# Feed-forward of a transformer block: a gate quad's seventh product behind the second product of what follows, and all products in one order

## The chip, the cores and the metric

The kernel runs on one core of a Trainium2 chip. The metric is the device time of one execution in microseconds (us), lower is better. Runs are told as a median with the lowest and the highest, and one execution is taken by the hardware profiler.

## The reference

The kernel computes one pre-norm encoder block for 2048 tokens of width 1024: a combined projection, two kinds of attention, an output projection, and a SwiGLU feed-forward of width 2816. The change is in the feed-forward alone, which is this part of the reference:

```
D_FF = ((8 * D_MODEL + 3 * 256 - 1) // (3 * 256)) * 256        # 2816
...
    u2 = rms_norm(h, norm2_w[l])
    gate = jnp.einsum('bsd,df->bsf', u2, w_gate[l])
    up = jnp.einsum('bsd,df->bsf', u2, w_up[l])
    h = h + jnp.einsum('bsf,fd->bsd', jax.nn.silu(gate) * up, w_down[l])
```

## The kernel before

Matrix products run on TensorE in f16, each operand split into a high and a low half, so that one product of two split blocks is three matmuls for each block of the contraction. A 2 by 2 block product is done with seven products and a chain of additions (Strassen's scheme in Winograd's form) and not with eight.

**The feed-forward's steps.** The tokens are two halves of 1024, the width 2816 is 11 groups of 256, so there are 22 steps (half, group), numbered 0 to 21 here. A step is a gate quad (`gate`, seven products of the step's gate weights `wg`), then an up quad (`up`, seven products of `wu`). Every product of a quad is 12 matmuls of 128x512 (`product`). Two steps after they were begun, two groups are multiplied into the result (`down`, "units"): this happens between the gate and the up of steps 2, 4, 6, 8, 10, then at step 11 for the single last group of the first half, then at steps 13, 15, 17, 19; the last three groups come at the end. A `down` has four blocks of 256 tokens (`j`), each with seven products of three matmuls for every unit, so 6 matmuls for two units. Its additions go into tiles `hs` (or `stages`) that are loaded from `hd` in memory (`load_hs`) and stored back there.

**Order of a quad.** With the names of `quad`: `pa` (first product), `p6`, `p7`, `pd`, a second product added into `pa`, `p4`, and the seventh, added into `pd`. Behind each stands an addition on VectorE or a copy on ScalarE: L1043, L1047, L1052, L1057 (reads `pd` after its first product), L1067, L1071 (reads `pd` after the seventh). The seventh can start when L1057 has read `pd`. A silu (L1083) in a gate, and L1103 in an up, follow. `hooks(n)` is called after the n-th product and advances the loading of weights.

**Loading of weights in the first half** (`load_ffn`, a generator that the hooks advance; in the second half ready weights are read back from memory): a DMA into one of two `stages`; ScalarE squares it into the one buffer `sq` (L954 for gate and up weights, L190 for down weights); a short group of matmuls, tile `fsc` (L963, or L183 through `across`), takes the sums over the partitions; VectorE makes the scale of them (L964, L175 to L205); then ScalarE, GpSimd and VectorE write the high and low halves (L216, L98, L221). The buffer `sq` is also the room for two combined blocks (`mix`), so the next square waits until L221 has read them. The up weights' `fsc` is traced at the gate's hook 2, the next step's gate weights' square at the gate's hook 6 and their `fsc` at its hook 7.

**PSUM.** Products and `fsc` tiles get their bank from `pst`, which counts: every fourth tile is of a pool of two, the other three of a pool of six.

**Who sets the order.** The program is traced as above, and then a list scheduler with a timeline of its own orders each engine's instructions: among those that it holds ready it takes the earliest traced, so a later product may be put ahead of an earlier one. `tc.issue_after(ins)` adds an edge: what the block traces on the engine of `ins` is issued behind `ins` (order only, no wait for its end). Before the change only the helpers (`fsc`, transposes `xtr`) carry such an edge, by `with behind():`, to `front[0]`, the last product's matmul traced so far; products carry none.

The changed functions and their callers:

Of the kernel before, what the change touches and what calls it, by code (L numbers as in the profile page):

```python
# [16 lines left out]
ALU = mybir.AluOpType  # L17
# [4 lines left out]
S, D, P = 2048, 1024, 128  # L22
# [18 lines left out]
CU = 3  # L41
# [18 lines left out]
def block(tc, a, out):  # L60
# [3 lines left out]
    with top:  # L64
# [64 lines left out]
        half = c1(2, "half")  # L129
# [744 lines left out]
        with ExitStack() as ph2:  # L874
# [150 lines left out]

            def product(ps_, wv, wo, X, xo, start, stop):
                q = 0
                for kt in range(4):
                    for xi, wi in ((0, 0), (1, 0), (0, 1)):
                        front[0] = PE.matmul(ps_[:].rearrange("p (t n) -> p t n", n=P), lhsT=wv[:, wo, wi, 128 * kt : 128 * kt + 128], rhs=X[xo][:, :, xi, kt, :], start=start and q == 0, stop=stop and q == 11, skip_group_check=not start).ins  # L1030
                        q += 1

            def quad(wv, X, tag, bufs, c11, hooks):
                def at(n):
                    hooks(n)

                def cst():
                    return fp.tile([P, 512], F32, tag=tag, bufs=bufs, name=nm(tag))

                pa = pst("pa")  # L1040
                product(pa, wv, 0, X, 0, True, True)
                u2 = cst()
                ACT.copy(u2[:], pa[:])  # L1043
                at(1)
                p6 = pst("pm")
                product(p6, wv, 4, X, 4, True, True)
                DVE.tensor_tensor(u2[:], p6[:], u2[:], ALU.add)  # L1047
                at(2)
                p7 = pst("pm")
                product(p7, wv, 6, X, 5, True, True)  # L1050
                u3 = cst()
                DVE.tensor_tensor(u3[:], p7[:], u2[:], ALU.add)  # L1052
                at(3)
                pd = pst("pd")
                product(pd, wv, 2, X, 2, True, True)
                c22 = cst()
                DVE.tensor_tensor(c22[:], pd[:], u3[:], ALU.add)  # L1057
                c11(1, 1, c22)
                at(4)
                product(pa, wv, 1, X, 1, False, True)  # L1060
                c11(0, 0, pa)
                note("D", 3000)
                note("A", 500)
                at(5)
                p4 = pst("pm")
                product(p4, wv, 3, X, 6, True, True)
                DVE.tensor_tensor(u3[:], u3[:], p4[:], ALU.subtract)  # L1067
                c11(1, 0, u3)
                at(6)
                product(pd, wv, 5, X, 3, False, True)  # L1070
                DVE.tensor_tensor(u2[:], u2[:], pd[:], ALU.add)  # L1071
                c11(0, 1, u2)
                at(7)

            def gate(W, X, hooks):
                sg = {}

                def on_gate(f, t, c):
                    if (f, t) == (0, 0):
                        s = fp.tile([P, 512], F32, tag="cg", bufs=5, name=nm("cg"))  # L1080
                    else:
                        s = c
                    ACT.activation(s[:], c[:], AF.Silu, scale=W["kg"][:])  # L1083
                    sg[f, t] = s

                quad(W["g"], X, "cg", 5, on_gate, hooks)
                note("A", 2000)
                return sg

            def up(W, X, sg, hooks, final=False):  # L1090
                if final:
                    act = stages[:].rearrange("p b n -> p (b n)").bitcast(F16)[:, :7168].rearrange("p (o s n) -> p o s n", o=7, s=2)
                else:
                    act = fp.tile([P, 7, 2, 512], F16, tag="act", bufs=2, name=nm("act"))

                def put(o, src):
                    ACT.copy(act[:, o, 0], src)  # L1097
                    note("A", 500)
                    tt(act[:, o, 1], src, act[:, o, 0], ALU.subtract, 512, LE)

                def on_up(f, t, c):
                    s = sg[f, t][:]
                    DVE.scalar_tensor_tensor(s, c[:], W["F"][:], s, op0=ALU.mult, op1=ALU.mult)  # L1103
                    if (f, t) != (0, 1):
                        put({(0, 0): 0, (1, 0): 1, (1, 1): 3}[f, t], s)
                        return
                    a11, a12, a21, a22 = (sg[k][:] for k in ((0, 0), (1, 0), (0, 1), (1, 1)))
                    s3 = fp.tile([P, 512], F32, tag="cu", bufs=CU, name=nm("cu"))
                    tt(s3[:], a11, a21, ALU.subtract, 512, SE)
                    tt(a21, a21, a22, ALU.add, 512, SE)  # L1110
                    put(2, a21)
                    tt(a11, a21, a11, ALU.subtract, 512, SE)
                    tt(a12, a12, a11, ALU.subtract, 512, SE)
                    put(6, a12)
                    put(4, a11)
                    put(5, s3[:])

                quad(W["u"], X, "cu", CU, on_up, hooks)
                note("D", 2440)
                return act  # L1120

# [6 lines left out]
                    SP.dma_start(h[q][:], hd[8 * half + 2 * j + q])  # L1128
                return h

            def down(half, units, hs, last, hook=None):
                kd = units[-1][0]["kd"]
                nu = len(units)

                def prod(po, ao, wo, j, start=True):
                    for u, (W, act) in enumerate(units):
                        for q, (xi, wi) in enumerate(((0, 0), (0, 1), (1, 0))):
                            front[0] = PE.matmul(po[:], lhsT=act[:, ao, xi, 128 * j : 128 * j + 128], rhs=W["d"][:, wo, wi, :], start=start and u == 0 and q == 0, stop=u == nu - 1 and q == 2, skip_group_check=not start).ins  # L1138

                def ust():  # L1140
                    return fp.tile([P, 512], F32, tag="cu", bufs=CU, name=nm("cu"))

                def acc(dst, po, src):
                    DVE.scalar_tensor_tensor(dst, po[:], kd[:], src, op0=ALU.mult, op1=ALU.add)  # L1144

                def first(j):
                    pa = pst("pd")
                    prod(pa, 0, 0, j)
                    return pa

                ahead = [first(j) for j in range(4)] if nu == 3 else []
                for j in range(4):
                    if j == 2 and hook is not None:
                        hook()
                    if j + 1 < 4:
                        hs.append(load_hs(half, j + 1, nu == 3, last))
                    h0, h1 = hs[j]
                    c11, c12, c21, c22 = h0[:, :512], h0[:, 512:], h1[:, :512], h1[:, 512:]
                    note("D", 3600)
                    note("A", 500)  # L1160
                    ae = "D" if last and j == 3 else AE
                    pa = ahead.pop(0) if ahead else first(j)
                    u2 = ust()
                    ACT.mul(u2[:], pa[:], kd[:])
                    pb = pst("pd")
                    prod(pb, 4, 4, j)
                    acc(u2[:], pb, u2[:])
                    pc = pst("pd")
                    prod(pc, 5, 6, j)
                    u3 = ust()  # L1170
                    acc(u3[:], pc, u2[:])
                    tt(c12, c12, u2[:], ALU.add, 512, ae)
                    pd = pst("pd")
                    prod(pd, 2, 2, j)
                    prod(pa, 1, 1, j, False)
                    acc(c22, pd, c22)
                    prod(pd, 6, 3, j, False)
                    acc(c11, pa, c11)
                    pe = pst("pd")
                    prod(pe, 3, 5, j)  # L1180
                    acc(c12, pd, c12)
                    acc(c21, pe, c21)
                    tt(c21, c21, u3[:], ALU.add, 512, ae)
                    tt(c22, c22, u3[:], ALU.add, 512, ae)
                    for q in range(2):
                        t = 8 * half + 2 * j + q
                        SP.dma_start(out[t * P : (t + 1) * P, :] if last else hd[t], hs[j][q][:])
# [69 lines left out]
            for i, (half, fg) in enumerate(steps):  # L1257
# [48 lines left out]
                        go("u")  # L1306
                    row(7 + s)

                sg = gate(W, X, in_gate)
                if not more:  # L1310
                    load_now(half, fg, "d", W)
                if due:
                    down(dh, units, hs, dh != half, lambda: go("g"))
                    units = []
                act = up(W, X, sg, in_up, not more)
                if more and steps[i + 1][0] == 1:
                    go("u", 9)
                units.append((W, act))
# [27 lines left out]
```

## Time and profile before

| | |
|---|---|
| median of 3 runs | 2686.87 us |
| lowest to highest | 2677.16 to 2687.23 us |
| profiled execution, its time | 2682.59 us |
| profiled execution, its span | 2680.8 us |
| first matmul of the feed-forward (gate of step 0) | 1427.2 us from the span's start |
| first matmul of its second half (gate of step 11) | 2059.6 us |

In the rows, PE is TensorE, DVE VectorE, ACT ScalarE, POOL GpSimd, SP the queue of most DMAs. A row of the timeline has start and length in us, then engine, line, operation, output and inputs with buffer numbers left out, shapes and a count; in brackets the idle time of the engine ahead of it and what ended it. Tiles of a quad are named `pa`, `pm` (for `p6`, `p7`, `p4`) and `pd`; those of `down` are all `pd`, on L1138, with inputs `wd,act`. A row of the waits has who waited for whom, us in total, times, and the longest. A row of the windows has the stretch, its length, each engine's busy time and count in the order PE, PE's weight loads, DVE, ACT, POOL, then the granted clock, the share of the DMA engines and GB/s.

### The profile page before, as it was taken

The page shows a single profiled execution, that of the slowest core. Times are in us where ns is not written, and L with a number is a line of the kernel's source. Part 1 is how long each engine was busy: PE and PEld are TensorE (multiplying, and loading weights), DVE is VectorE, ACT ScalarE, POOL GpSimd, SP SyncE. Part 2 cuts the span into 40 slices and gives each one's busy share as a digit, 9 for nine tenths or more (in the row PEclk, how much of TensorE's full clock was granted, in tenths as well). Part 3 has the DMA queues.
Part 4 walks back from the last instruction along what each step waited for, and adds up shares of the span by engine and source line. Part 5 has one row for each costly group of instructions (what it writes and reads, how often), then busy time and mean ns, then how long its engine had stood idle before and what let it go on. Part 6 is the DMA issues. An engine that isn't in the chain of part 4 may idle for free. (4 is left out here: it accounts for less than half of the span.)

```text
span 2680.8 us, 50579 instructions
## 1 busy us (share of the span) xinstructions
PE 2492.4 (93%) x19628; PEld 1498.6 (56%) x19628; DVE 1932.7 (72%) x3711; ACT 1347.0 (50%) x2487; POOL 1489.1 (56%) x1098
## 2 busy tenths in 40 slices
PE   6998989888988989889989899999999999999999
PEld 4655656577776776557775344444444444444444
DVE  6898969898989989877766868777685544444434
ACT  4665656567978878665644535344352112111121
POOL 2578667667767766546764656565564232322323
PEclk9999999999999999999999899999999999999999
DMA  6777697767998979987897574665649743635532
GB/s 222 213 162 181 146 200 168 179 143 184 193 179 179 185 160 209 210 191 217 218 285 282 208 250 178 255 226 202 245 183 346 293 177 143 233 141 186 195 111 95
DMA packets 619585, 534.41 MB, mean 199 GB/s; under 512 B 480640, under 2 KB 548224, under 8 KB 609104
## 3 DMA queue, kind: packets, MB, share of 16 engines
q1 hardware_dynamic: 617520, 529.09, 69.9%
q8 instruction: 154, 2.52, 0.4%
q0 software_dynamic: 512, 1.36, 0.2%
q14 instruction: 87, 0.71, 0.1%
q10 hardware_dynamic: 1312, 0.72, 0.1%
HBM read 261.08 MB, written 147.32 MB: 152 GB/s over the span
## 5 line engine op out<-in xcount | busy, mean ns | idle before, releaser
L98 POOL TENSOR_TENSOR s<-z,s 128x1024 f16<-128x1024 f32 (+7 forms) x288 | 472.0, 1647 | 142.5 <-ACT s L89 109.8
L507 PE MATMUL sc<-kT,qT 128*128 128x512 f16 (+3 forms) x1520 | 382.0, 353 | 53.3 <-DVE z L623 19.3
L622 DVE TENSOR_TENSOR_SCAN z<-z,sc 128x512 f32<-128x512 f32 (+3 forms) x320 | 352.8, 1112 | 58.6 <-ACT sc L620 38.0
L1138 PE MATMUL pd<-wd,act 128*128 128x512 f16 x1764 | 390.9, 379 | 1.2 <-DVE cg L1071 1.2
L326 PE MATMUL pj<-w,xt 128*128 128x384 f16 x1920 | 352.2, 331 | 18.8 <-ACT xt L683 6.9
L1030 PEld LDWEIGHTS <-wg 128*128 128x128 f16 x1848 | 182.0, 99 | 230.2 <-issue 16.4
L518 PE MATMUL yp<-v,aT 128*128 128x64 f16 (+1 forms) x4896 | 269.8, 204 | 41.6 <-DMA aT<-s 40.2
L518 PEld LDWEIGHTS <-aT 128*128 128x128 f16 x4896 | 237.5, 99 | 120.4 <-DMA aT<-s 52.5
L1030 PEld LDWEIGHTS <-wu 128*128 128x128 f16 x1848 | 180.7, 98 | 218.0 <-issue 2.6
L98 POOL TENSOR_TENSOR act<-cg,act 128x512 f16<-128x512 f32 x112 | 148.5, 1337 | 262.9 <-ACT act L1097 150.8
L1138 PEld LDWEIGHTS <-act 128*128 128x128 f16 x1764 | 172.8, 98 | 209.4 <-issue 2.8
L326 PEld LDWEIGHTS <-xt 128*128 128x128 f16 x1920 | 187.3, 99 | 147.5 <-issue 21.4
L89 ACT CAST s<-z 128x128 f16<-128x128 f32 (+7 forms) x215 | 173.1, 809 | 134.1 <-DMA aT<-s 40.5
L98 POOL TENSOR_TENSOR hs<-hs,cu 128x512 f32<-128x512 f32 x99 | 130.9, 1328 | 171.3 <-DVE hs L1144 70.8
L619 ACT ACTIVATE z<-sc,c 128x512 f32<-128x512 f32 (+3 forms) x320 | 210.7, 663 | 25.6 <-PE sc L507 11.7
L1097 ACT CAST act<-cg 128x512 f16<-128x512 f32 x126 | 77.3, 616 | 238.4 <-DVE cg L1103 162.7
L507 PEld LDWEIGHTS <-qT 128*128 128x128 f16 x1520 | 128.4, 99 | 121.0 <-DVE z L623 23.0
L832 PE MATMUL po<-wo,mt 128*128 128x256 f16 x1536 | 180.7, 277 | 13.9 <-DVE xf L835 8.4
L1030 PE MATMUL pm<-X,wu 128*128 128x512 f16 x792 | 180.4, 379 | 1.3 <-DVE wu L221 1.3
L1030 PE MATMUL pm<-X,wg 128*128 128x512 f16 x792 | 181.3, 382 | 0.0
L342 PE MATMUL pj<-xt,w 128*128 128x128 f16 x2304 | 175.0, 220 | 6.7 <-DVE v L364 5.7
L1144 DVE SCALAR_TENSOR_TENSOR hs<-pd,c,hs 128x512 f32<-128x512 f32 x136 | 99.0, 747 | 109.6 <-PE pd L1138 83.1
(266 smaller groups left out, 4737.6 us busy)
## 6 DMA issues: line engine op xcount, KB each, us to landing
xt<-xs SPq DMA_DIRECT2D x112, 512.0 KB, 4.3
hs<-hd SPq DMA_DIRECT2D x68, 512.0 KB, 4.5
hd<-hs SPq DMA_DIRECT2D x56, 512.0 KB, 4.7
split<-wg SPq DMA_DIRECT2D x11, 1792.0 KB, 7.8
split<-wu SPq DMA_DIRECT2D x11, 1792.0 KB, 6.7
split<-wd SPq DMA_DIRECT2D x11, 1792.0 KB, 7.2
wg<-split SPq DMA_DIRECT2D x11, 1792.0 KB, 7.3
wd<-split SPq DMA_DIRECT2D x11, 1792.0 KB, 12.2
```

Source lines behind the costliest of these rows:

```text
L89: ACT.copy(dst, src)
L98: (DVE if e == "D" else POOL).tensor_tensor(dst, a_, b_, op)
L326: PE.matmul(pj[:, :384], lhsT=xv[:, xi, kt, :], rhs=G["w"][:, wi, kt, :], start=n == 0, stop=n == 23)
L342: PE.matmul(o, lhsT=x_ if c == 2 else w_, rhs=w_ if c == 2 else x_, start=n == 0, stop=n == 23)
L507: last = PE.matmul(sc[:, : 128 * w].rearrange("p (t n) -> p t n", n=P), lhsT=G["q"][i // 4][:, a_, i % 4, :], rhs=G["k"][q][:, b_, 0:w, :] ...
L518: PE.matmul(yp[:, y0 : y0 + wd], lhsT=aT[:, a_, :], rhs=v[:, v_ : v_ + wd], start=start and j == 0 and q == 0, stop=stop and j == nb - 1 a ...
L619: ACT.activation(om[:, lo:hi], sc[:, :w], AF.Sigmoid, scale=G["nkz"][:])
L622: DVE.tensor_tensor_scan(ov, ov, sc[:, :w], om[:, hi : hi + 1], op0=ALU.mult, op1=ALU.bypass)
L832: PE.matmul(po[:, sl], lhsT=mt[:, kt, P * xi : P * xi + P], rhs=wos[2 * h + n][wi][:, kt, :], start=q == 0, stop=q == 23)
L1030: front[0] = PE.matmul(ps_[:].rearrange("p (t n) -> p t n", n=P), lhsT=wv[:, wo, wi, 128 * kt : 128 * kt + 128], rhs=X[xo][:, :, xi, kt, : ...
L1138: front[0] = PE.matmul(po[:], lhsT=act[:, ao, xi, 128 * j : 128 * j + 128], rhs=W["d"][:, wo, wi, :], start=start and u == 0 and q == 0, s ...
L1144: DVE.scalar_tensor_tensor(dst, po[:], kd[:], src, op0=ALU.mult, op1=ALU.add)
```

## The change

`quad` hands out its seventh product as a function; with `late` (gates alone) it does not call it. The next `down` calls it at its first block `j == 0` behind its second product, or, in a step without one, the next `up` calls it behind its `p6`. Hook 7 of a gate is now called before the seventh product has been traced. Every product, of quads and of `down`, is traced inside `with behind():`, so each matmul of it has an edge to the last matmul of the product traced before it. The count of tiles in `pst` stays as it was.

```diff
             def product(ps_, wv, wo, X, xo, start, stop):
                 q = 0
-                for kt in range(4):
-                    for xi, wi in ((0, 0), (1, 0), (0, 1)):
-                        front[0] = PE.matmul(...).ins
-                        q += 1
+                with behind():
+                    for kt in range(4):
+                        for xi, wi in ((0, 0), (1, 0), (0, 1)):
+                            last = PE.matmul(...)
+                            q += 1
+                front[0] = last.ins
...
-            def quad(wv, X, tag, bufs, c11, hooks):
+            def quad(wv, X, tag, bufs, c11, hooks, before=None, late=False):
...
                 DVE.tensor_tensor(u2[:], p6[:], u2[:], ALU.add)
+                if before is not None:
+                    before()
                 at(2)
...
                 at(6)
-                product(pd, wv, 5, X, 3, False, True)
-                DVE.tensor_tensor(u2[:], u2[:], pd[:], ALU.add)
-                c11(0, 1, u2)
+
+                def seventh():
+                    product(pd, wv, 5, X, 3, False, True)
+                    DVE.tensor_tensor(u2[:], u2[:], pd[:], ALU.add)
+                    c11(0, 1, u2)
+
+                if not late:
+                    seventh()
                 at(7)
+                return seventh
...
-                quad(W["g"], X, "cg", 5, on_gate, hooks)
+                seventh = quad(W["g"], X, "cg", 5, on_gate, hooks, None, True)
                 note("A", 2000)
-                return sg
+                return sg, seventh
...
                 def prod(po, ao, wo, j, start=True):
-                    for u, (W, act) in enumerate(units):
-                        for q, (xi, wi) in enumerate(((0, 0), (0, 1), (1, 0))):
-                            front[0] = PE.matmul(...).ins
+                    with behind():
+                        for u, (W, act) in enumerate(units):
+                            for q, (xi, wi) in enumerate(((0, 0), (0, 1), (1, 0))):
+                                last = PE.matmul(...)
+                    front[0] = last.ins
...
                     acc(u2[:], pb, u2[:])
+                    if before is not None and j == 0:
+                        before()
                     pc = pst("pd")
...
-                sg = gate(W, X, in_gate)
+                sg, seventh = gate(W, X, in_gate)
...
-                    down(dh, units, hs, dh != half, lambda: go("g"))
-                    units = []
-                act = up(W, X, sg, in_up, not more)
+                    down(dh, units, hs, dh != half, lambda: go("g"), seventh)
+                    units, seventh = [], None
+                act = up(W, X, sg, in_up, not more, seventh)
```

More of the change, by code (lines that the diff above doesn't have):

```diff
@@ L1027, in product @@
                 q = 0
-                for kt in range(4):
-                    for xi, wi in ((0, 0), (1, 0), (0, 1)):
-                        front[0] = PE.matmul(ps_[:].rearrange("p (t n) -> p t n", n=P), lhsT=wv[:, wo, wi, 128 * kt : 128 * kt + 128], rhs=X[xo][:, :, xi, kt, :], start=start and q == 0, stop=stop and q == 11, skip_group_check=not start).ins
-                        q += 1
-            def quad(wv, X, tag, bufs, c11, hooks):
+                with behind():
+                    for kt in range(4):
+                        for xi, wi in ((0, 0), (1, 0), (0, 1)):
+                            last = PE.matmul(ps_[:].rearrange("p (t n) -> p t n", n=P), lhsT=wv[:, wo, wi, 128 * kt : 128 * kt + 128], rhs=X[xo][:, :, xi, kt, :], start=start and q == 0, stop=stop and q == 11, skip_group_check=not start)
+                            q += 1
+                front[0] = last.ins
+            def quad(wv, X, tag, bufs, c11, hooks, before=None, late=False):
                 def at(n):
@@ L1084, in on_gate, with up @@
                     sg[f, t] = s
-                quad(W["g"], X, "cg", 5, on_gate, hooks)
+                seventh = quad(W["g"], X, "cg", 5, on_gate, hooks, None, True)
                 note("A", 2000)
-                return sg
-            def up(W, X, sg, hooks, final=False):
+                return sg, seventh
+            def up(W, X, sg, hooks, final=False, before=None):
                 if final:
@@ L1116, in on_up @@
                     put(5, s3[:])
-                quad(W["u"], X, "cu", CU, on_up, hooks)
+                quad(W["u"], X, "cu", CU, on_up, hooks, before)
                 note("D", 2440)
@@ L1129, in load_hs, with down @@
                 return h
-            def down(half, units, hs, last, hook=None):
+            def down(half, units, hs, last, hook=None, before=None):
                 kd = units[-1][0]["kd"]
@@ L1135, in prod @@
                 def prod(po, ao, wo, j, start=True):
-                    for u, (W, act) in enumerate(units):
-                        for q, (xi, wi) in enumerate(((0, 0), (0, 1), (1, 0))):
-                            front[0] = PE.matmul(po[:], lhsT=act[:, ao, xi, 128 * j : 128 * j + 128], rhs=W["d"][:, wo, wi, :], start=start and u == 0 and q == 0, stop=u == nu - 1 and q == 2, skip_group_check=not start).ins
+                    with behind():
+                        for u, (W, act) in enumerate(units):
+                            for q, (xi, wi) in enumerate(((0, 0), (0, 1), (1, 0))):
+                                last = PE.matmul(po[:], lhsT=act[:, ao, xi, 128 * j : 128 * j + 128], rhs=W["d"][:, wo, wi, :], start=start and u == 0 and q == 0, stop=u == nu - 1 and q == 2, skip_group_check=not start)
+                    front[0] = last.ins
                 def ust():
```

## The prediction

> **What bounds the kernel now.** I read the windows over the feed-forward first, then TensorE's waits from 1427 to the end.
>
> ```profile
> 1550.00:2070.00 520.00, 515.16 (x2447) 240.35 (x2446) 382.02 (x581) 223.94 (x266) 296.59 (x212) 1.00 0.64 234
> 2070.00:2100.00 30.00, 30.00 (x141) 13.60 (x140) 19.65 (x29) 6.08 (x9) 12.01 (x10) 1.00 1.00 403
> 2100.00:2621.00 521.00, 521.00 (x2416) 236.16 (x2415) 218.59 (x284) 93.51 (x149) 151.94 (x120) 1.00 0.47 173
> ...
> PE pd L1030 <- DVE cg L1057: 8.9, 3, 5.5
> PE fsc L963 <- ACT sq L954: 5.9, 1, 5.9
> PE pd L1138 <- DVE cg L1071: 1.2, 1, 1.2
> PE pd L1030 <- DMA X<-xcd: 1.0, 1, 1.0
> ```
>
> TensorE bounds the feed-forward: from 2100 it has no idle time (521.00 of 521.00 us), and from 1550 to 2070 it lacks 4.8 of 520. The four waits shown, 17.0 us, are most of what can be won there. The first is the one that the late seventh product addresses. VectorE, though, is 73% busy in the first half (382.02 of 520), where it writes weights, against 42% in the second (218.59 of 521). TensorE hides that only if it has something else to do while VectorE is late, so I read what it does then. This is the gate of step 5, and the moment at which its neighbours' squares run:
>
> ```profile
> 1712.39 2.75 PE L1030 MATMUL pd<-X,wu 128*128 128x512 f16 x12
> 1714.98 2.75 PE L1030 MATMUL pa<-X,wg 128*128 128x512 f16 x12
> 1721.24 1.04 PE L963 MATMUL fsc<-sq,ones 128*128 128x256 bf16 x8
> 1722.11 2.75 PE L1030 MATMUL pm<-X,wg 128*128 128x512 f16 x12
> 1731.39 0.59 PE L1030 MATMUL pm<-X,wu 128*128 128x512 f16 x2
> 1732.65 1.69 PE L1030 MATMUL pm<-X,wu 128*128 128x512 f16 x7 [0.66 <-DVE wu L221]
> 1734.17 2.75 PE L1030 MATMUL pd<-X,wg 128*128 128x512 f16 x12
> 1736.76 0.81 PE L1030 MATMUL pm<-X,wu 128*128 128x512 f16 x3
> 1737.41 1.04 PE L963 MATMUL fsc<-sq,ones 128*128 128x256 bf16 x8
> ...
> 1494.14 1.91 ACT L954 ACTIVATE sq<-stages 128x2048 bf16<-128x2048 f32 x1 [2.30 <-DVE wu L221]
> 1547.41 1.91 ACT L954 ACTIVATE sq<-stages 128x2048 bf16<-128x2048 f32 x1 [0.94 <-DVE wu L221]
> 1620.94 1.91 ACT L954 ACTIVATE sq<-stages 128x2048 bf16<-128x2048 f32 x1 [0.61 <-DVE wu L221]
> 1735.06 1.91 ACT L954 ACTIVATE sq<-stages 128x2048 bf16<-128x2048 f32 x1 [0.48 <-DVE wu L221]
> 1778.65 1.91 ACT L954 ACTIVATE sq<-stages 128x2048 bf16<-128x2048 f32 x1 [1.17 <-DVE wu L221]
> 1966.79 1.91 ACT L954 ACTIVATE sq<-stages 128x2048 bf16<-128x2048 f32 x1 [0.48 <-DVE wu L221]
> ```
>
> A product takes 2.59 us (1714.98 less 1712.39), an `fsc` 0.87. The `fsc` at 1737.41 starts 0.44 after its square ends (1735.06 + 1.91 = 1736.97), and the square has waited for VectorE's weight writing. TensorE is not idle meanwhile: at 1731.39 it has taken a product of the up (`p7`) ahead of the gate's seventh, of the `fsc` and of the up's `pa` and `p6`. That is the scheduler's reordering, and it is what keeps 1550 to 2070 so full. The overtaker is always a tile of the two-bank pool: in the program's order no tile of the six-bank pool is opened ahead of an earlier traced tile of that pool, here `fsc`, then `pa`.
>
> **The change part by part.** *The order, at the gate's end.* With edges, `pa` of the up follows `p4`, and the seventh follows the up's `p6`. Hook 7 is now traced ahead of all three, so the `fsc` comes between `p4` and `pa`, and where `fsc` and `pa` are both of the six-bank pool, `pa` cannot open first. So TensorE has no product to run until the square is done. From the end of the last up (1712.39 + 2.59 = 1714.98) it has six products and an `fsc`, 6 x 2.59 + 0.87 = 16.4 us, and the square ends 1736.97 - 1714.98 = 22.0 later: 5.6 us idle. Against now, the loss is the work that was ahead of the `fsc` and no longer is, less the time by which the `fsc` started behind its square. Here 24 matmuls (the seventh and 2 + 7 + 3 of `p7`), 5.18, less 0.44, 4.7 us. The same points in the other first-half gates, with their seventh products:
>
> ```profile
> 1491.13 4.76 PE L1030 MATMUL pd<-X,wg 128*128 128x512 f16 x12 [5.47 <-DVE cg L1057]
> 1496.16 2.75 PE L1030 MATMUL pm<-X,wu 128*128 128x512 f16 x12
> 1498.75 1.04 PE L963 MATMUL fsc<-sq,ones 128*128 128x256 bf16 x8
> ...
> 1544.03 2.75 PE L1030 MATMUL pd<-X,wg 128*128 128x512 f16 x12
> 1549.37 1.03 PE L963 MATMUL fsc<-sq,ones 128*128 128x256 bf16 x8
> ...
> 1619.11 2.75 PE L1030 MATMUL pd<-X,wg 128*128 128x512 f16 x12
> 1623.86 1.04 PE L963 MATMUL fsc<-sq,ones 128*128 128x256 bf16 x8
> ...
> 1773.91 4.13 PE L1030 MATMUL pd<-X,wg 128*128 128x512 f16 x12 [3.30 <-DVE cg L1057]
> 1780.78 1.04 PE L963 MATMUL fsc<-sq,ones 128*128 128x256 bf16 x8
> ...
> 1965.90 2.75 PE L1030 MATMUL pd<-X,wg 128*128 128x512 f16 x12
> 1969.13 1.04 PE L963 MATMUL fsc<-sq,ones 128*128 128x256 bf16 x8
> ```
>
> In step 1 the seventh and the up's `p7` (1496.16) stand ahead of the `fsc`, and in steps 2, 6 and 9 the timeline has the seventh and as many matmuls of what follows, in part ahead of the seventh, 5.18 us each; the square ends 2.70, 0.05, 0.22 and 0.43 earlier: 2.5, 5.1, 5.0 and 4.8. In step 3 `pa` is the two-bank tile and still opens first, `p6` is held: 2.59 less 1.01, 1.6. Step 7 has the same place in the count and gets the same 1.6. In steps 4 and 8 the `fsc` itself is the two-bank tile, at step 0 and step 10 nothing is held: none. Sum 25.3 us. This contains the waits for L1057 in steps 1 and 6 (5.47 and 3.30): they go, but the time until the square passes idle in their place. Each of the other ends hands its time on, since TensorE works without a pause between them.
>
> *The clock.* The seventh behind the 5.47 us wait took 4.76 us for 2.75, behind the 3.30 us wait 4.13: 2.0 and 1.4 lost. I put 2.0 to each of the five waits of that size (steps 1, 2, 5, 6, 9): 10.0. The rows hold these spells at 1491 and 1773 already, but ahead of the `fsc`, so they are in the comparison above and the new ones are extra. The Trainium skill, "TensorE: Matmul & The Clock Gate", Part 1, section "What's actually happening", has the array at half rate after an idle window of about 3.4 us and until about as long a busy one; by it a spell would cost an estimated 1.7 us, five 8.5. The trace agrees in kind, but a wait of 3.30 already did it.
>
> *The half change.* At step 11 the products' input `X` is replaced, and the DMA engines are full (share 1.00 in the second window).
>
> ```profile
> 2069.96 4.05 PE L1138 MATMUL pd<-wd,act 128*128 128x512 f16 x18
> 2073.86 2.75 PE L1030 MATMUL pa<-X,wg 128*128 128x512 f16 x12
> 2088.10 2.75 PE L1030 MATMUL pd<-X,wg 128*128 128x512 f16 x12
> ...
> L1225 SPq DMA_DIRECT2D X<-xcd x1: 319/319/319, 2064.5 to 2064.5; - x1
> ...
> DMA to landing us min/median/max: 21.1/21.1/21.1
> ...
> DVE hs L1144 <- DMA hs<-hd: 26.3, 13, 4.3
> ...
> 2282.55 0.75 DVE L1144 SCALAR_TENSOR_TENSOR hs<-pd,c,hs 128x512 f32<-128x512 f32 x1 [0.55 <-PE pd L1138]
> ```
>
> Now `down` products, already runnable, fill the time until each `X` is there. In order, the fifth gate product waits from 2069.96 to 2073.86, 3.9 us. Then come `p4` (to 2079.04) and two `down` products of three matmuls, 1.3, to 2080.34, and the seventh waits for the last `X`, 2064.5 + 21.1 = 2085.6: 5.3. With 2.0 for the clock at each, 13.2 us.
>
> *The downs.* Their third-to-last product needs L1144 to have read `pd`; the scheduler now puts it behind later ones, and the edges forbid that. In the second half the cover holds: at 2282.55 L1144 starts when its product ends and takes 0.75, and the product between is six matmuls, 1.30 us by the 2.59 for twelve. So nothing there. In the first half L1144 also waits for `hs`, 26.3 us in 13 times, 2.0 each, which then stops TensorE. The bounds are nothing (the delayed product comes three products earlier, so the stores that free `hs` come up to 3.9 us earlier) and 4.3 each, 21.5. I take the mean wait for each of five downs: 10.
>
> *What goes.* The wait for `X` at step 0, 1.0 us, is hidden by the two products now ahead of the seventh. The seventh's own later end costs nothing: its silu is used last in the up, five products later. Its addition L1071 now stands among the additions of what follows, which wait behind it on VectorE only where the seventh itself waits, at step 11, where TensorE stands still as well. Holding the gate weights for two products more delays the next load (SP) by up to 5.2 us, and in the second half an up's seven products, 18.1 us, cover that.
>
> The sum: 25.3 + 10.0 + 13.2 + 10 - 1.0 = 57.5 us on the profiled execution's 2682.6: 2740 us. That execution is 4.3 us under the median of the runs and within their spread.
>
> **The rivals.** *Faster.* The waits for L1057, L1071 and the first `X` go (8.9 + 1.2 + 1.0), with their slow clock (2.0 + 1.4), and order costs nothing: 2668 us. That needs each square some 5 us earlier. For it: VectorE's order is made anew, and it no longer has the seventh's L1071 there. Against: that is one addition, and VectorE is behind with weight writing, not with additions. *No change.* The new waits are shared out: the squares come about 2.5 us earlier and no clock is lost, downs and half change cost little; within 0.5%, about 2684. *Worse.* Every first-half down loses the longest wait, 4.3, and a slow spell of 2.0: 31.5 in place of 10, 2762 us; it decides if the loads of `hs` still follow late stores. *The edges change nothing*, since products ran in order anyway: excluded by 1731.39.
>
> **How the numbers follow.** A measurement of this kernel can tell about 0.5%, 13.4 us, from no change. Chances: the forecast 0.62, worse 0.13, no change 0.13, faster 0.12. So faster by over 0.5% 0.12, within 0.13, slower 0.75. The forecast's own range is 2698 (half of 25.3 and one `X` wait, no clock, no down) to 2765 (downs at their bound and the rest as summed, with a spell at each end). To hold the time 8 times in 10 the range takes in the no-change case: 2680 to 2772.
>
> **What would show it.** The waits of TensorE should have `fsc` behind L954 at the top, about 5 us each at steps 1, 2, 5, 6 and 9, with a granted clock near 0.5 behind them; L1057 of a gate should be gone; `pd` on L1030 and `pa` should wait for `X` near 2100; the stretch of the second half behind step 13 should be as full as now. A window over the first half with no more idle time than now would prove me wrong, as would a `pa` of an up ahead of its `fsc` at step 5.

## The result: 2.8% slower, and the profile after

The changed kernel takes 2756.46 us (median of 6 runs, 2753.19 to 2761.42), the kernel before 2681.03 in the 6 runs beside it: a ratio of 1.028, 95% interval 1.0262 to 1.0297. The profiled execution took 2757.03 us (span 2755.3), 74.4 more than that of before. The forecast was 2740, a sum of 57.5.

First the windows over the feed-forward, cut so that both kernels have the same instructions in each (the "x" in brackets counts the matmul records): its first half with the half change, then as long a stretch of the second half. Before:

```profile
1427.20:2105.00 677.80, 657.35 (x3113) 307.31 (x3112) 498.73 (x746) 298.07 (x360) 378.48 (x266) 0.99 0.65 239
2105.00:2665.00 560.00, 560.00 (x2596) 253.82 (x2595) 234.55 (x305) 98.81 (x157) 169.64 (x134) 1.00 0.45 166
```

After; the last row is the stretch that was quoted of before, at the same times:

```profile
1426.20:2178.80 752.60, 679.61 (x3113) 314.09 (x3111) 497.74 (x746) 298.75 (x360) 377.09 (x266) 0.95 0.60 218
2178.80:2738.80 560.00, 560.00 (x2596) 253.85 (x2595) 236.46 (x305) 98.78 (x157) 168.38 (x133) 1.00 0.46 162
...
1550.00:2070.00 520.00, 476.49 (x2194) 219.55 (x2193) 348.31 (x527) 212.70 (x250) 275.01 (x193) 0.96 0.55 200
```

The two kernels do the same 3113 matmul records, the changed one in 752.60 us and not in 677.80: 74.8 more, the whole loss. Two columns split it. TensorE's idle time went from 677.80 - 657.35 = 20.45 us to 752.60 - 679.61 = 72.99, 52.5 more. Its busy time for the same matmuls went up by 22.3, which is the lower granted clock (0.99, then 0.95). The second half behind it hasn't changed at all: 560.00 busy of 560.00 in both. VectorE does the same work in both (498.73, 497.74): it is not slower, it is waited for.

What TensorE waited for most, from 1426 to 2180 in the changed kernel:

```profile
PE fsc L963 <- ACT sq L954: 37.5, 12, 5.5
PE pd L1149 <- DVE hs L1156: 16.7, 10, 5.3
PE xtr L1227 <- DVE bx L229: 7.0, 1, 7.0
PE pa L1031 <- DMA X<-xcd: 5.1, 1, 5.1
PE pd L1031 <- DMA X<-xcd: 2.3, 1, 2.3
PE pm L1031 <- DMA X<-xcd: 1.7, 1, 1.7
```

The waits for a chain tile of the gate (L1057 before, L1061 here) are gone, as the change meant. In their place `fsc` stands at the top with 37.5 us.

The gate's end of step 5, the same place that the prediction showed of before, on TensorE, and its square on ScalarE:

```profile
1744.64 2.75 PE L1031 MATMUL pm<-X,wg 128*128 128x512 f16 x12
1752.87 1.87 PE L963 MATMUL fsc<-sq,ones 128*128 128x256 bf16 x8 [5.48 <-ACT sq L954]
1754.53 4.11 PE L1031 MATMUL pa<-X,wu 128*128 128x512 f16 x12
1758.48 2.75 PE L1031 MATMUL pm<-X,wu 128*128 128x512 f16 x12
1761.07 2.75 PE L1031 MATMUL pd<-X,wg 128*128 128x512 f16 x12
...
1750.91 1.91 ACT L954 ACTIVATE sq<-stages 128x2048 bf16<-128x2048 f32 x1 [0.47 <-DVE wu L221]
```

Behind `p4` (1744.64) nothing may run but `fsc` (`pa` is held behind it, as forecast), and its square ends at 1752.82. Then come `pa`, `p6` and the seventh, as traced. The 5.48 us of idle time were forecast as 5.6. The `fsc` took 1.87 where one at full clock takes 1.04, and `pa` 4.11 for 2.75: 2.2 us lost to the clock.

To see where the loss sits by step, I took the end of each step's up from both timelines of TensorE. The increments of the difference, in us, from the start of the feed-forward:

| step | 0 | 1 | 2 | 3 | 4 | 5 | 6 | 7 | 8 | 9 | 10 | 11 | 12 to 21 |
|---|---|---|---|---|---|---|---|---|---|---|---|---|---|
| changed kernel | -3.0 | 3.5 | 5.1 | 1.6 | 9.5 | 4.0 | 9.2 | 2.1 | 11.3 | 4.6 | 9.6 | 17.2 | 0.0 |
| forecast | -1.0 | 4.5 | 9.1 | 1.6 | 2.0 | 6.7 | 9.0 | 1.6 | 2.0 | 6.8 | 2.0 | 13.2 | 0 |

The even steps from 2 to 10 have a `down`. The forecast's row is its terms laid out by step: gate's end, 2.0 of clock where it had put one, and 2.0 for a `down`. Steps 4, 8 and 10 stand out. A step's loss is not only its own stalls, though. Before, the scheduler ran 12 to 14 matmuls of the next gate ahead of the end of the ups of steps 1, 5 and 9 (14 of them, 3.0 us, in step 5: the `pa` and `pd` on `wg` from 1746.05 to 1751.23); in order none are. So the row counts steps 1, 5 and 9 too low by up to 3.0 us and steps 2, 6 and 10 too high by as much.

### The profile page after: what moved, and what is told of

It is laid out like the page before. It is cut to its first block, busy times and chain, and to the rows that moved or that the text cites. A ratio compares the mean times of both kernels' runs of the same rounds, so it can differ in the third digit from the quotient of the medians.

```text
span 2755.3 us, 50645 instructions
## 1 busy us (share of the span) xinstructions
PE 2517.9 (91%) x19628; PEld 1506.7 (55%) x19628; DVE 1935.1 (70%) x3711; ACT 1346.7 (49%) x2487; POOL 1488.6 (54%) x1098
## 4 chain that ended last, share of the span: by engine, by line
PE 36%; DVE 9%; DMA 6%; issue 4%; POOL 3%; ACT 3%; SPq 0%; DVEq 0%; POOLq 0%; ACTq 0%
PE pd L1149 11%; PE pm L1031 9%; PE pd L1031 6%; PE pa L1031 6%; PE po L832 2%; DMA hd<-hs 2%; DVE z L622 1%; DVE wd L221 1%; DVE wu L221 1%; DMA X<-xcd 1%; POOL s L98 1%; DMA aT<-s 1%; ACT sq L954 1%; DMA hs<-hd 1%; PE pj L326 1%
## 5 line engine op out<-in xcount | busy, mean ns | idle before, releaser
L1149 PE MATMUL pd<-wd,act 128*128 128x512 f16 x1764 | 396.8, 383 | 18.3 <-DVE hs L1156 16.7
L543 DVE TENSOR_SCALAR_CACHE_REDUCE z<-sc,c 128x512 f32<-128x512 f32 (+3 forms) x256 | 160.9, 646 | 17.9 <-PE sc L507 16.8
```

Of the source, the lines that this page charges most:

```text
L543: DVE.tensor_scalar(z[:, lo : lo + f], sc[:, :f], kz_d[:], None, op0=ALU.mult, op1=ALU.max, accum_out=mx[:, m, nx : nx + 1])
L1149: last = PE.matmul(po[:], lhsT=act[:, ao, xi, 128 * j : 128 * j + 128], rhs=W["d"][:, wo, wi, :], start=start and u == 0 and q == 0, stop= ...
```

## The experiments

The theory: the fixed order of the products costs the time, since TensorE then stands at whatever is late (an `fsc`, an `hs`, an `X`), and the late seventh product by itself does little. The rival: the late seventh costs it, with its bank, its weights and its hook held longer. The first four kernels split the change. "Feed-forward" below is the difference from before over the feed-forward alone in the profiled executions, 74.8 in the changed kernel.

**The late seventh alone.**

```diff
 def product(...):
-                with behind():
+                with nullcontext():
 ...
 def prod(...):
-                    with behind():
+                    with nullcontext():
```

> The seventh product late, no edges between products. If the edges cost the time (my theory): no stall of TensorE at fsc of several us, time as before or a little under it, 2670 to 2690, since the waits for the gate's L1057 (8.9 us) go. If the late seventh costs it (a PSUM bank, the gate weights and a chain tile held longer, hook 7 called before it): near the changed kernel, 2735 to 2760.

2678.88 us against 2684.79, ratio 0.9982 (0.9967 to 0.9996); feed-forward -1.7. Without the order the rival falls. The expected gain did not come in full: of the 8.9 us of waits for L1057 5.5 remain (L1061), and one wait for `fsc` of 5.1 us remains, where the kernel before had one of 5.9. TensorE at the same place of step 5, in this kernel:

```profile
1736.03 0.59 PE L1031 MATMUL pm<-X,wu 128*128 128x512 f16 x2
1737.29 1.68 PE L1031 MATMUL pm<-X,wu 128*128 128x512 f16 x7 [0.67 <-DVE wu L221]
1738.81 2.75 PE L1031 MATMUL pd<-X,wg 128*128 128x512 f16 x12
1741.40 0.81 PE L1031 MATMUL pm<-X,wu 128*128 128x512 f16 x3
1742.05 1.04 PE L963 MATMUL fsc<-sq,ones 128*128 128x256 bf16 x8
```

This is, row for row, the order of before: the scheduler again takes products of the up ahead of the `fsc`. Where a product is traced matters little if the scheduler may move it.

**The edges alone.**

```diff
-                quad(W["g"], X, "cg", 5, on_gate, hooks, None, True)
+                quad(W["g"], X, "cg", 5, on_gate, hooks, None, False)
 ...
-                sg, seventh = gate(W, X, in_gate)
+                sg, seventh = gate(W, X, in_gate)[0], None
```

> The seventh in its old place, every product behind the one before. If the edges cost the time: the downs of the first half keep their 9.5 to 11.3 us each (50), the half change most of its 17, and the gates' stalls shrink by the one product that is again ahead of fsc (2.6 us each) but the waits for L1057 come back: 2740 to 2765. If the late seventh costs it: 2675 to 2695.

2742.28 us, ratio 1.0219 (1.0198 to 1.0241); feed-forward 57.2. The edges make the kernel slower without the late seventh. Under edges the late seventh costs 74.8 - 57.2 = 17.6 more, so the two are not independent. Here the seventh stands ahead of the `fsc` again and covers part of its wait: in steps 5 and 9 TensorE waits 1.70 us for a chain tile and 1.02 for the `fsc`, in place of 5.48 and 5.46. All waits for L963 are 17.5 us in place of 37.5; those for L1061 are back (12.4).

**Edges on one kind of product**, with the late seventh: on the quads' alone (`prod` without `behind`), then on the downs' alone (`product` without it).

> Late seventh, edges on the quads' products alone; the products of a down may be reordered among themselves. If the downs lose their time by their own order: the gates' 16 to 25 us stay and the downs' 50 go: 2695 to 2720. If the downs lose only because squares and loads come late behind the gates' stalls: still over 2735.

2705.02 us, ratio 1.0088 (1.0065 to 1.0112); feed-forward 26.7. The first of TensorE's waits there:

```profile
PE fsc L963 <- ACT sq L954: 28.6, 8, 5.5
```

> Late seventh, edges on the downs' products alone; each of these still follows the last product traced before it. If the downs lose their time by their own order (the reload of hs): 40 to 55 us remain, gates without stall at fsc, 2720 to 2740. If not: 2675 to 2700.

2730.01 us, ratio 1.0173 (1.0147 to 1.0199); feed-forward 47.3:

```profile
PE fsc L963 <- ACT sq L954: 16.4, 8, 5.1
PE pd L1149 <- DVE hs L1156: 14.3, 8, 5.1
PE pd L1031 <- DVE cg L1061: 9.8, 4, 3.6
PE pa L1031 <- DMA X<-xcd: 3.7, 2, 3.5
```

I expected no stall at `fsc` here; there are 16.4 us, 6.1 of which the late seventh alone has too. In total the two parts add up, though not wait by wait (28.6 and 16.4 at `fsc`, 37.5 with both). Against the late seventh alone, the quads' edges cost 26.7 + 1.7 = 28.4 us, the downs' 49.0, together 77.4; both at once cost 76.5. By step, the quads' edges make the losses of the steps without a `down` (3.4, 1.6, 4.7, 3.8, 3.3) and of step 10 (8.4); the downs' edges make those of steps 4 (9.7) and 8 (11.1) and all of step 11 (17.5; with the quads' edges alone it is 0.0, though the products of its quads are in order there too).

**`fsc` behind the seventh.** Hook 7 is called behind the seventh product and not ahead of it.

```diff
                 def seventh():
                     product(pd, wv, 5, X, 3, False, True)
 ...
+                    at(7)
                 if not late:
                     seventh()
-                at(7)
```

> As the changed kernel, but hook 7 of a gate is called behind the seventh product, so that fsc is traced and ordered two products (5.2 us) later, with the seventh and a product of what follows ahead of it. If the stalls at fsc come from the place of fsc in the order: 1.6 to 5 us less at steps 1, 2, 3, 5, 6, 7 and 9, 12 to 22 in all, 2734 to 2745. If the squares come later for their own reasons (VectorE) and drag the weights behind them: still over 2750.

2752.28 us, ratio 1.026 (1.0239 to 1.0281); feed-forward 69.0. I expected 12 to 22 us less; it was 5.8. The place of `fsc` does matter: its waits at the gates' ends of steps 2, 3, 5, 6, 7 and 9 are 5.76 us together in place of 20.46. They are gone in steps 2, 3, 6 and 7; in steps 5 and 9 the square is still late, and of 5.48 and 5.46 us 2.89 and 2.87 remain:

```profile
1760.73 1.03 PE L963 MATMUL fsc<-sq,ones 128*128 128x256 bf16 x8 [2.89 <-ACT sq L954]
```

But other waits grew. Those for `hs` went from 16.7 to 21.1 us, those for `fsc` in steps 4 and 8 from 1.55 to 2.94 and 2.84. In step 1 the `fsc` waits 6.22 in place of 2.98, while the wait of 7.0 at `xtr` is gone. In step 2 the `fsc` of the up weights waits longer than any in the changed kernel:

```profile
1537.95 1.87 PE L963 MATMUL fsc<-sq,ones 128*128 128x256 bf16 x8 [9.54 <-ACT sq L954]
1528.59 2.19 ACT L216 ACTIVATE wd<-stages,c 128x1024 f16<-128x1024 f32 x2 [0.33 <-DMA xcd<-b]
```

The later `fsc` at the gate's end of step 1 explains little of this: counted from the feed-forward's start, it begins less than half a us later than in the changed kernel (1497.17 and 1492.71; starts 1430.21 and 1426.20). The writing of the down weights between them, which holds `sq`, begins 7.4 us later (1528.59 and 1517.17) and was last released by a DMA that stores the next half's `X`. So this kernel shows that the place of `fsc` sets part of its wait. That a later `fsc` drags the weights behind it, the other reading, it does not show.

**The downs: third-to-last product without an edge.**

```diff
-                def prod(po, ao, wo, j, start=True):
-                    with behind():
+                def prod(po, ao, wo, j, start=True, free=False):
+                    with nullcontext() if free else behind():
...
-                    front[0] = last.ins
+                    front[0] = front[0] if free else last.ins
...
-                    prod(pd, 6, 3, j, False)
+                    prod(pd, 6, 3, j, False, True)
```

> As the changed kernel, but the third-to-last product of a down's block (the second into pd) has no edge to either side and may slide behind later ones. If the downs lose their time because that product waits for L1156 and so for the reload of hs (my theory): of the 33 us that downs with edges cost in steps 2 to 10 at most 10 stay, and part of step 11's 17: 2715 to 2735. If any order inside a down costs it: over 2745.

2723.03 us, ratio 1.0154 (1.0135 to 1.0172); feed-forward 44.8. No wait for `hs` is left among TensorE's waits, and the steps with a `down` lose 22.6 in place of 44.7 (steps 4 and 8: 1.7 each). Step 11 loses 9.9 in place of 17.2.

**The downs: without the stores.** The `down`s of steps 2 to 10 leave out the store of `hs`, so their sums are lost.

```diff
-                    for q in range(2):
+                    for q in range(0 if half == 0 and nu == 2 else 2):
                         t = 8 * half + 2 * j + q
                         SP.dma_start(out...
```

> As the changed kernel, but the two-unit downs of the first half leave out the store of hs to hd (so their sums are lost), and the loads of hs need not wait for it. If the stall is the chain store, load, addition, product: steps 2 to 10 lose at most 10 of the downs' 33, step 11 is as in the changed kernel: 2725 to 2740. If the loads are late for another reason (queue, full DMA engines, VectorE): over 2748.

2727.15 us, ratio 1.0168 (1.015 to 1.0186); feed-forward 43.2. The `down` of step 4, in the changed kernel and then without the stores:

```profile
1672.26 11.82 PE L1149 MATMUL pd<-wd,act 128*128 128x512 f16 x54
1685.17 9.22 PE L1149 MATMUL pd<-wd,act 128*128 128x512 f16 x42 [1.09 <-DVE hs L1156]
1699.13 13.50 PE L1149 MATMUL pd<-wd,act 128*128 128x512 f16 x54 [4.74 <-DVE hs L1156]
```

```profile
1684.94 20.88 PE L1149 MATMUL pd<-wd,act 128*128 128x512 f16 x96 [1.08 <-DVE hs L1156]
```

The 4.74 us wait and the slow spell behind it (13.50 us for as many matmuls as had taken 11.82) go with the stores. That shows the chain store, reload, addition, product. The total came as expected, but not its parts: step 11 lost 4.8 us and not 17.2, which I had not expected. SP's queue says why. The first `X` load of the half change stands in it behind the last reloads of step 10's `down`; here before, in the changed kernel and without the stores:

```profile
2031.56 1.59 SPq L1128 DMA_DIRECT2D hs<-hd  x2
2033.85 2.08 SPq L1187 DMA_DIRECT2D hd<-hs  x2
2039.72 1.54 SPq L1128 DMA_DIRECT2D hs<-hd  x2
...
2044.03 0.32 SPq L1225 DMA_DIRECT2D X<-xcd  x1
```

```profile
2100.59 0.32 SPq L1138 DMA_DIRECT2D hs<-hd  x1
2101.01 0.38 SPq L1201 DMA_DIRECT2D hd<-hs  x1
2106.09 0.32 SPq L1138 DMA_DIRECT2D hs<-hd  x1
...
2106.93 0.42 SPq L1239 DMA_DIRECT2D X<-xcd  x1
```

```profile
2063.25 21.02 SPq L1138 DMA_DIRECT2D hs<-hd  x6
2084.41 8.09 SPq L1239 DMA_DIRECT2D X<-xcd  x4
```

Before, two reloads and two stores go out together, every 8.2 us. In the changed kernel SP issues one store, waits for it, issues one reload: 5.5 us for each tile here (2100.59 to 2106.09), 5.7 for the one before, 11.2 for two. Step 11's gate starts at 2059.60, 2116.18 and 2100.0: the first `X` is issued 15.6, 9.3 and 15.6 us ahead of it. In the kernel of the experiment before, where only the third-to-last product has lost its edge, SP issues pairs again, and the first `X` goes out 15.6 us ahead of the gate (2073.37 and 2088.93). So the alternation goes with that edge; how it comes about was not followed further.

**Step 11's `down` free.**

```diff
-                    with behind():
+                    with nullcontext() if nu == 1 else behind():
```

> As the changed kernel, but the single-unit down of step 11 has no edges. If down products that could run during the waits for X are what the edges took from the half change: the 17 us of step 11 go, 2736 to 2744. If the half change loses by the order of the gate's and the up's products: over 2750.

2741.53 us, ratio 1.0222 (1.0202 to 1.0242); feed-forward 61.2, step 11 3.9. `X` is issued as late as in the changed kernel, but other products fill the time. So the half change needs two things to lose its 17 us: `X` late, and nothing else allowed to run. With `X` in time and the order kept it lost 9.9 and 4.8 in the two experiments before, with `X` late and the `down` free 3.9.

**Without the squares and their `fsc`**, with edges and then without. The gate and up weights of groups 1 to 10 take the scale of group 0; the count of tiles goes on as if the `fsc` were there.

```diff
-                    else:
+                    elif fg == 0:
                         ACT.activation(sq[:], st, AF.Square)
 ...
+                    known = nme != "d" and fg > 0
+                    if known:
+                        pst_n[0] += 1
+                    else:
+                        pt = pst("fsc")
 ...
+                    if known:
+                        r, p, sW = scales[0][nme]
+                    else:
+                        scale_end(...)
```

> As the changed kernel, but gate and up weights of groups 1 to 10 take the scale of group 0: their square on ScalarE, their fsc on TensorE and the chain that makes the scale on VectorE are left out. If the stalls are TensorE standing in order at fsc while the weights behind it are in time: the 37.5 us of waits at L963 and their slow clock (some 12) go and the downs' and step 11's stay: 2698 to 2718. If VectorE's writing of weights is too slow whatever TensorE's order is: the waits move to the products' wg and wu behind L221, over 2735.

2722.06 us, ratio 1.0142 (1.0125 to 1.0159); feed-forward 38.0. All of the 37.5 us at L963 are gone, but the time is 4 us over what I expected, as waits grew elsewhere:

```profile
PE pd L1156 <- DVE hs L1163: 22.0, 11, 6.2
PE pd L1156 <- ACT cg L1100: 14.2, 2, 7.3
```

> The same part left out, late seventh, no edges between products. If the order is what makes an fsc cost anything: only the fsc's own 20 times 0.87 us on TensorE and the remaining waits go, 2655 to 2675. If the squares hold the first half in any order: under 2650.

2671.26 us, ratio 0.9959 (0.9943 to 0.9974); feed-forward -16.9, 15.2 less than the late seventh alone, and the 20 `fsc` groups themselves are 20 x 0.87 = 17.4 us. So without edges the squares cost TensorE no more than their own matmuls; with edges, leaving them out saved 74.8 - 38.0 = 36.8. The difference, 21.6 us, is what the order adds to them, net of the waits that grew.

The only kernel that does all the work and beats both is the late seventh alone, by 0.18%, less than the half per cent that tells two kernels apart here.

## Why the prediction was right, and where its sizes were off

The sign and the place were right, and so was the mechanism in kind: all the loss lies in steps 1 to 11, TensorE stands at `fsc`, `hs` and `X`, and the second half is untouched. The sum was 17.3 us short (74.8 for 57.5). By its two kinds of cost, idle time was forecast at 57.5 - 14.0 = 43.5 and was 52.5; the clock at 14.0 and was 22.3. The terms of the idle time, from TensorE's rows of both timelines:

| idle time, us | before | after | change | forecast |
|---|---|---|---|---|
| gate's end (`fsc` of hook 7, and what stood there before) | 11.4 | 26.5 | 15.1 | 25.3 |
| `fsc` of the up weights (hook 2) | 5.9 | 11.0 | 5.1 | none |
| `xtr` of step 1 | 0 | 7.0 | 7.0 | none |
| downs of steps 2 to 10 | 0 | 16.0 | 16.0 | 10 |
| `down` of step 11 | 0 | 2.4 | 2.4 | none |
| `X` at the half change | 0 | 9.1 | 9.1 | 9.2 |
| `X` at step 0, and the rest | 3.0 | 1.0 | -2.0 | -1.0 |
| sum (20.45 and 72.99 with rounding and small gaps) | 20.3 | 73.0 | 52.7 | 43.5 |

One term was too large and four were missing or too small, so that the total came closer than its parts: that is in part luck.

- *Gate's end.* The stalls were 2.98, 3.43, 1.46, 5.48, 2.40, 2.23 and 5.46 us in steps 1, 2, 3, 5, 6, 7 and 9, 23.4 together, and 1.55 each in steps 4 and 8, which had been put at nothing: three products of the `down` and the seventh are ahead of the `fsc` there, and that is still not enough. The forecast of 25.3 looks met, but it was net of the waits that go, 11.4 us by the rows of before, so the net 15.1 is what it must be held against. In steps 1 and 6 the forecast let the whole wait for L1057 (5.47 and 3.30) pass idle at the `fsc` on top of the loss, some 8 us each; they were 2.98 and 2.40, since TensorE had already stood 6.99 us at the transposes of step 1 and 3.71 at the up weights' `fsc` of step 6. Of the five stalls of "about 5 us each" two were of that size. The sequence was as argued: in steps 3 and 7 `pa` opens first, in the others `fsc`.
- *A term that was not there.* I costed the `fsc` at hook 7 and not the one at hook 2, of the up weights, inside the gate. It has only `pa` and `p6` ahead of it and waited 3.58, 3.71 and 3.72 us in steps 2, 6 and 10. In step 2 it had waited before as well (5.88, the 5.9 in the prediction's table of waits); in steps 6 and 10 it is new. Before, two more products of the gate, `pd` and the second into `pa`, ran ahead of it in step 10:

```profile
1988.79 2.75 PE L1030 MATMUL pm<-X,wg 128*128 128x512 f16 x12
1991.38 2.32 PE L1030 MATMUL pd<-X,wg 128*128 128x512 f16 x10
1993.54 2.75 PE L1030 MATMUL pa<-X,wg 128*128 128x512 f16 x12
1996.13 1.04 PE L963 MATMUL fsc<-sq,ones 128*128 128x256 bf16 x8
```

  and now, in the changed kernel:

```profile
2044.81 1.87 PE L963 MATMUL fsc<-sq,ones 128*128 128x256 bf16 x8 [3.72 <-ACT sq L954]
2046.46 4.91 PE L1031 MATMUL pm<-X,wg 128*128 128x512 f16 x12
```

  The 3.72 us and 3.0 of slow clock (1.87 for 1.04, 4.91 for 2.75) are most of step 10's 9.6, for which the forecast had only the `down`'s 2.0; the kernel with edges on quads alone has them too (8.4). But the lost cover is not the whole cause. With edges alone the same two products are ahead of this `fsc`, and in step 6 it does not wait. Its row there, and ScalarE's writing of the next gate weights, first with edges alone, then in the changed kernel:

```profile
1777.41 1.03 PE L963 MATMUL fsc<-sq,ones 128*128 128x256 bf16 x8
1755.48 2.19 ACT L216 ACTIVATE wg<-stages,c 128x1024 f16<-128x1024 f32 x2 [1.35 <-issue]
```

```profile
1763.86 2.19 ACT L216 ACTIVATE wg<-stages,c 128x1024 f16<-128x1024 f32 x2 [4.59 <-PE pd L1031]
```

  Gate and up weights share two buffers (tag `wgu`), so the next gate weights go where the late seventh still reads. Both kernels run the `fsc` of these weights at the same time (1752.95 and 1752.87). Their writing starts 2.6 us after the square's end with edges alone and 11.0 us after it in the changed kernel, at the end of the seventh, and the next square follows 8.2 us later (1769.35 against 1761.18). The prediction had put the seventh's later end at nothing, and had weighed the longer hold of the gate weights only for the second half. In the first half, under edges, that step was wrong.
- *Downs.* The mechanism, the third-to-last product behind L1156 and so behind the reload, is shown by the two experiments on it. The size was not: forecast 10 us in all, 2.0 each, with a bound of 4.3. The waits for `hs` in steps 2, 4, 6, 8 and 10 were 1.83, 5.83, 1.91, 6.39 and 0, together 16.0, and steps 4 and 8 pay a slow spell besides. The wrong step was to take the mean of VectorE's 13 waits for one wait of each `down`: a `down` has four blocks, and in steps 2, 4, 6 and 8 two of them waited.
- *Half change.* Waits for `X` 1.7 + 5.1 + 2.3 = 9.1, forecast 3.9 + 5.3 = 9.2. That the sums agree is luck: the waits are at other products and for a reason that was only half seen, as I had the lost cover and not SP's queue. The clock and the waits of step 11's own `down` (2.4) make the rest of the 17.2.
- *Clock.* A spell was forecast at 2.0 us; by the rows with lengthened matmuls it cost 1.7 to 3.0 (2.2 in step 5). There were eleven in the changed kernel's feed-forward and three in that of before; the forecast added seven. The Trainium skill, "TensorE: Matmul & The Clock Gate", Part 1, section "What's actually happening", has the clock gate look at a free-running window of about 3.4 us. By it a wait under 3.4 us need not slow anything, and waits of 2.40 and 2.23 did not; but slow matmuls also followed a wait of 2.98 (with one of 6.99 shortly ahead of it) and one of 2.30 (last section), which the length of the wait alone doesn't explain.
- *Steps 0 and 1.* The gain of step 0 was 3.0 and not 1.0. The wait of 7.0 us at the transposes of step 1 (L1227) was not named; its loss is inside that step's 3.5, against 4.5 forecast.

Of the rivals, "worse" (2762) lies nearer to the measured 2756 than the forecast of 2740 does. It had one part right, the downs, but the wrong amount for each. "Faster" and "no change" fail by the same row: the 1744.64 product of step 5 with nothing allowed behind it. The recorded range of 2680 to 2772 held the case of no change too, so that the time lies in it says little. Its upper ends don't follow from the terms: with the downs at 21.5 and the rest as summed they give 69.0 us, 2752; 2765 has 13 us more in spells that are not listed, and 2772 has no working.

## What to carry to other kernels

A fixed order on an engine that never idles removes the cover for everything that is sometimes late; look first at what overtakes what today, since each overtaking can be a wait that the order will expose, and go through every late producer of the loop, not only the one beside the edit. A product that is moved back also holds its operands longer: ask who writes into that buffer next. For a term that repeats, count how often the wait can occur in one pass before taking a mean of the waits of another engine. And an order on one engine can change the order in a DMA queue that several streams share: check what is queued behind it.

## What the runs showed of the hardware

I had not expected a wait of 2.30 us to slow the clock when one of 2.40 doesn't. In step 11 of the changed kernel it follows one of 5.10 by 12 us:

```profile
2133.68 5.30 PE L1031 MATMUL pa<-X,wg 128*128 128x512 f16 x12 [5.10 <-DMA X<-xcd]
2138.78 3.15 PE L1031 MATMUL pm<-X,wg 128*128 128x512 f16 x12
2141.76 1.46 PE L1149 MATMUL pd<-wd,act 128*128 128x512 f16 x6
2145.51 4.45 PE L1031 MATMUL pd<-X,wg 128*128 128x512 f16 x12 [2.30 <-DMA X<-xcd]
```

In the kernel without squares a product even took 4.09 us for 2.75 behind a wait of 1.29, with waits of 0.78 and 1.32 shortly ahead of it and three matmuls between. Whether short waits add up or these only fell in an unlucky place, no run here settles.
